# A two-layer hybrid trunk on one core: queries turned one place later, one weighing ahead of the next unit's sums, a head's norm behind the low part of the head ahead, and the FFN's norm rows a triple later

## The chip, the core and the metric

The kernel runs on one core of a Trainium2 chip. Five engines work side by side, each through its own list of instructions, in order: TensorE (PE, matrix products and transposes), VectorE (DVE), ScalarE (ACT), GpSimd (POOL) and SyncE (SP, which starts the weight transfers). They wait for each other through semaphores. The metric is the device time of one execution in microseconds (us); the lower, the better.

## The reference

The input is x, 512 tokens by 1024 features in float32. Two layers are applied. Layer 0 is a Mamba-2 mixer and a ConvFFN; then one shared K/V projection is made; layer 1 is differential attention over it and a second ConvFFN. The parts that the change touches:

```python
def conv_ffn(x, ln_g, up_w, conv_w, conv_b, down_w):
    u = causal_dwconv(rms_norm(x, ln_g) @ up_w, conv_w, conv_b)
    gate, up = u[..., :FFN_DIM], u[..., FFN_DIM:]
    return (jax.nn.silu(gate) * up) @ down_w
...
    q = (rms_norm(x, ln_g) @ q_w).reshape(b, s, ATT_HEADS, 2, ATT_HEAD_DIM)
    q = rms_norm(q, q_norm_g)
    lam = jnp.exp(jnp.sum(lv[0] * lv[1])) - jnp.exp(jnp.sum(lv[2] * lv[3])) + lam_init
...
        logits = jnp.einsum('bqhcd,bkhcd->bhcqk', qblk, k).astype(jnp.float32) * scale
        logits = logits + bias[None, :, None]
        logits = jnp.where(dist >= 0, logits, -jnp.inf)
        p = jax.nn.softmax(logits, axis=-1)
        attn = p[:, :, 0] - lam * p[:, :, 1]
        return jnp.einsum('bhqk,bkhd->bqhd', attn.astype(v.dtype), v)
...
    o = rms_norm(o, subln_g) * (1.0 - lam_init)
    return o.reshape(b, s, V_TOTAL) @ out_w
```

There are 8 attention heads, each with two softmax maps of width 64 and a value width of 128; the FFN is 2816 wide. Before the mixers and FFNs stands an RMS norm whose factor per token is taken out of the product: the product is made with the raw stream, and its result is multiplied by the factor.

## The kernel before

**Products.** Every float32 operand is split in a high and a low part, and each product is three matmuls, high by high, high by low and low by high (`mm3`, L196 to L198; with the tokens on the output's partitions in `proj`, L997 to L999). Such a group is called a triple here. Features lie on the 128 partitions in 8 blocks, the 512 tokens along the free axis. Weights come in chunks by SP's queue into `wr_...`; ACT makes the high part `wh_...` (L147, L165), DVE the low part `wl_...` (L151, L166), two chunks ahead of their use.

**PSUM.** Eight banks: four called "mm" for the long products, four called "aux" for everything short (transposes, logits, values). Each kind is handed out in a ring, so a new use of a bank waits until the engine that reads its last use is done.

**The FFN.** It goes through 22 pairs of blocks, gate `g` and up `u`. A block is 8 triples into an mm bank (`ps_g...`, `ps_u...`), then DVE multiplies by the norm row (`uu`/L874), and three taps of a convolution follow. The norm row is made inside the first pair: `tr_nf` (sum of squares, transposed, then the inverse root on DVE, L428) is turned by four transposes into `al_nf` (L455) and copied by ACT into `nr_f` (L503). On PE the four transposes of `al_nf` stand within the first u block.

**Attention.** k, q and v are projected in two halves of four heads (k0, q0, v0, k1, q1, v1). A finished q projection is squared and summed, gets its norm (L1019 to L1028, tile `knq`), and is transposed in four banks `ktq` (L1035), each evacuated by ACT into `qT` (L1036). When this happens is said by a pair of places, such as `((0, 3), (2, 1))`: the first two banks behind block (k0 = 0, bank 3) of the projection that follows, the next two behind (2, 1). One bank of a step of two features' blocks is six matmuls.

A head is three units, `PARTS = ((0, 1), (2,), (3,))`, of the token blocks given; unit 6_1 is head 6, part 1. A unit runs through: logits (PE L1079 into two aux banks; DVE's maxima L1085, negated at L1088; ACT's exponentials L1093, which also sum), weighing (`weigh`: DVE's reciprocal `rc` L1100, `sm` L1102, and the difference of the two maps `lg` L1106), turning (PE's transposes `at` L1114, copied by ACT L1115) and values (PE `po` L1125, ACT `ot` L1128). After its last unit a head gets its norm (`normed_out`: squares `osq` by ACT at L1135, DVE's sum `so` L1136, the inverse root L434 to L439 with two small ACT instructions at L435 and L436, and the scaling `ot` L1138) and later its transposition (`turned_out`: PE `oT` L1144, ACT's high part `oh` L1147, DVE's low part `ol` L1148), then the output projection, whose results DVE adds to the stream (`xT`, L510).

**What sets the order.** In the attention stage PE's order is written out by hand: between the steps of the units a generator `fill` puts pieces of the projections. The other engines' order comes from a scheduler at build time, which goes by its own estimates of when inputs are ready; `tc.issue_after(x)` puts what stands under it behind x in that order. Each engine then follows its list strictly.

Of the kernel before, what the change touches and what calls it, by code (L numbers as in the profile page):

```python
# [39 lines left out]
def trunk_kernel(ctx: ExitStack, tc, x, ssm_ln_g, ssm_in_w, ssm_conv_w, ssm_conv_b, ssm_dt_bias,  # L40
# [443 lines left out]
    class Norm:  # L484
# [15 lines left out]
        def row(self):  # L500
            ps = along_tokens(self.col(), "n" + self.name)
            r = self.pl.tile([P, T], F32, tag="nr", name="nr_" + self.name)
            act.activation(r, ps, AF.Copy)  # L503
            return r
# [351 lines left out]
    def ffn(l, norm, bp, gnext, nnext):  # L856
        with tc.tile_pool(name="ffn_h%d" % l, bufs=1) as hp, tc.tile_pool(name="ffn%d" % l, bufs=1) as fp:
            rr = []

            def u_block(j, p):  # L860
                key = "%s%d_%d" % ("gu"[j], l, p)
                wh, wl = chunk(key)
                ps = mm_bank("ps_" + key)
                for k in range(KB):
                    mm3(ps, wh[:, k, :], wl[:, k, :], xgh[k], xgl[k], k == 0, k == KB - 1)
                if not rr:
                    rr.append(norm.row())
                r = rr[0]
                col = lambda t: cf[l][:, 88 * j + 22 * t + p:88 * j + 22 * t + p + 1]
                u = fp.tile([P, T], F32, tag="u", name="u" + key, bufs=3)  # L870
                v = fp.tile([P, T], F32, tag="v%d" % j, name="v" + key, bufs=3)
                if nnext is None and key in ("g1_1", "u1_1"):
                    residual(j)
                dve.tensor_tensor(out=u, in0=ps, in1=r, op=ALU.mult)  # L874
                act.activation(v, u, AF.Identity, bias=col(3), scale=col(2))
                for s in range(1, 3):
                    dve.scalar_tensor_tensor(out=v[:, s:], in0=u[:, :T - s], scalar=col(2 - s),
                                             in1=v[:, s:], op0=ALU.mult, op1=ALU.add)
                return v
# [50 lines left out]
            for p0, p1 in ((0, HALF), (HALF, NPAIR)):  # L930
                last = p1 == NPAIR
                hh, hl = [], []
                for p in range(p0, p1):
                    ga = u_block(0, p)
                    act.activation(ga, ga, AF.Silu)
                    up = u_block(1, p)
# [28 lines left out]
    with tc.tile_pool(name="att_o", bufs=1) as op_, tc.tile_pool(name="att", bufs=1) as ap:  # L965
# [23 lines left out]
        def proj(key, evac):  # L989
            pss = [mm_bank("ps_%s_%d" % (key, b)) for b in range(NT)]  # L990
            for k0 in range(0, KB, 2):
                wh, wl = chunk("%s_%d" % (key, k0))
                for b in range(NT):
                    ts = slice(b * P, (b + 1) * P)
                    for k in range(k0, k0 + 2):
# [3 lines left out]
                        pe.matmul(pss[b], xgl[k][:, ts], wh[:, k - k0, :], start=False, stop=sp_)  # L999
                    if b % 2:  # L1000
                        if late and late[0][0] == (k0, b):
                            late.pop(0)[1]()
# [47 lines left out]
        class Unit:  # L1050
# [45 lines left out]
            def weigh(self):  # L1096
# [7 lines left out]
                for j, i in enumerate(self.ii):  # L1104
                    c = slice(self.off[j], self.off[j] + (i + 1) * P)
                    dve.scalar_tensor_tensor(out=p[0][:, c], in0=p[1][:, c], scalar=sm[:, j, 1:2],  # L1106
                                             in1=p[0][:, c], op0=ALU.mult, op1=ALU.add)
# [32 lines left out]
        def turned_out(h, st):  # L1140
            ot = st["ot"]
            ps = aux_bank("oT%d" % h)
            for i in range(NT):
# [4 lines left out]
            dve.scalar_tensor_tensor(out=ol_, in0=ps, scalar=c2[:, 50:51], in1=oh_.bitcast(F32),  # L1148
                                     op0=ALU.mult, op1=ALU.subtract)
# [48 lines left out]
        with tc.manual_schedule(engines={mybir.EngineType.PE}):  # L1198
            run(qk("k0", kT[0], 48, ((2, 1), (2, 3))))
            run(qk("q0", qT[0], 49, ((0, 3), (2, 1))))  # L1200
            fill = chain(vproj("v0", 0), qk("k1", kT[1], 48, ((0, 3), (2, 3))), qk("q1", qT[1], 49, ((0, 3), (2, 1))), vproj("v1", 1),
# [7 lines left out]
            ots = []  # L1209
# [3 lines left out]
            def values(t):  # L1213
                u = us[t]
                u.values()
                if u.part == len(PARTS) - 1:
                    normed_out(u.h, u.st)
                    ots.append([t + 4 + u.h // 4, u])
# [26 lines left out]
            for places in [(2, 2), (2, 2), (2, 2), 2, 2, (2, 2), 2, 2, 2, 1, 1, 1, 2, 1, 2, 1, 2, 1, 2, 2, 1, 1, 1]:  # L1245
                if isinstance(places, tuple):
                    weigh_to(t)
                    turn_to(t - 1)
                    values_to(t - 2)
                    turn_to(t)  # L1250
                    next(fill)
                    out_of(t + 1)
                    values_to(t)
                    next(fill)
# [9 lines left out]
                if t < n:  # L1264
                    us[t].logits()
                weigh_to(t)
                values_to(t - 2)
                for i in range(places):
                    next(fill)
                    if i == 0 and (places > 1 or t > n):  # L1270
                        out_of(t)
                t += 1
# [40 lines left out]
```

## Time and profile before

| what | value |
|---|---|
| time, median of 3 runs | 1351.42 us (1350.94 to 1352.56) |
| profiled execution | 1352.13 us, its span 1350.4 us |
| PE busy | 1342.4 us, 99% of the span |
| DVE, ACT, POOL busy | 68%, 48%, 8% |
| last chain: PE, DVE, ACT | 93%, 3%, 2% |

A row of the timeline reads: start in us, length in us, engine, line, operation, output<-inputs, shapes, count; in brackets how long the engine idled before it, and whose instruction ended that. Lengths of matmuls are modelled and overlap the next one's start, so distances are taken from start to start. Line numbers are those of the kernel before; in the changed one the same instructions of the attention stand some ten lines further on.

### The profile page before, as it was taken

The page shows a single profiled execution, that of the slowest core. Times are in us where ns is not written, and L with a number is a line of the kernel's source. Part 1 is how long each engine was busy: PE and PEld are TensorE (multiplying, and loading weights), DVE is VectorE, ACT ScalarE, POOL GpSimd, SP SyncE. Part 2 cuts the span into 40 slices and gives each one's busy share as a digit, 9 for nine tenths or more (in the row PEclk, how much of TensorE's full clock was granted, in tenths as well). Part 3 has the DMA queues.
Part 4 walks back from the last instruction along what each step waited for, and adds up shares of the span by engine and source line. Part 5 has one row for each costly group of instructions (what it writes and reads, how often), then busy time and mean ns, then how long its engine had stood idle before and what let it go on. Part 6 is the DMA issues. An engine that isn't in the chain of part 4 may idle for free.

```text
span 1350.4 us, 16886 instructions
## 1 busy us (share of the span) xinstructions
PE 1342.4 (99%) x6423; PEld 1097.3 (81%) x6423; DVE 915.0 (68%) x1525; ACT 646.2 (48%) x1060; POOL 106.3 (8%) x142
## 2 busy tenths in 40 slices
PE   9999999999999999999999999999999999999998
PEld 7878788888888888888888887777888888888887
DVE  4989888788877774267754556778777773367743
ACT  5696553742444442234433556777654442134430
POOL 6230400200110000000001200000110000000000
PEclk9999999999999999999999999999999999999999
DMA  7453433432333333333323422221232332333322
GB/s 204 143 166 90 138 109 110 133 94 71 94 94 94 94 98 105 94 94 94 100 80 102 133 78 89 69 86 36 76 92 87 103 94 94 94 104 99 94 94 78
DMA packets 179825, 134.98 MB, mean 100 GB/s; under 512 B 6492, under 2 KB 163552, under 8 KB 179744
## 3 DMA queue, kind: packets, MB, share of 16 engines
q1 hardware_dynamic: 173872, 120.73, 29.7%
q0 software_dynamic: 4592, 12.08, 2.8%
q10 hardware_dynamic: 1280, 1.10, 0.2%
q8 instruction: 50, 0.82, 0.2%
q14 instruction: 31, 0.25, 0.1%
HBM read 131.64 MB, written 2.25 MB: 99 GB/s over the span
## 4 chain that ended last, share of the span: by engine, by line
PE 93%; DVE 3%; ACT 2%; issue 1%; DMA 0%; POOL 0%; SPq 0%; ACTq 0%; DVEq 0%
PE ps_g L197 6%; PE ps_g L198 6%; PE ps_g L196 6%; PE ps_u L198 6%; PE ps_u L196 6%; PE ps_u L197 6%; PE ps_in L196 4%; PE ps_in L197 4%; PE ps_in L198 4%; PE ps_d L198 3%; PE ps_d L196 3%; PE ps_d L197 3%; PE ps_d L915 3%; PE ps_d L914 3%; PE ps_d L913 3%; PE ps_o L197 2%
## 5 line engine op out<-in xcount | busy, mean ns | idle before, releaser
L196 PE MATMUL ps_u<-xgh,wh_u 128*128 128x512 f32 x352 | 137.6, 391 | 0.0
L197 PE MATMUL ps_g<-xgl,wh_g 128*128 128x512 f32 x352 | 137.2, 390 | 0.0
L196 PE MATMUL ps_g<-xgh,wh_g 128*128 128x512 f32 x352 | 137.2, 390 | 0.0
L198 PE MATMUL ps_u<-xgh,wl_u 128*128 128x512 f32 x352 | 137.2, 390 | 0.0
L198 PE MATMUL ps_g<-xgh,wl_g 128*128 128x512 f32 x352 | 137.2, 390 | 0.0
L197 PE MATMUL ps_u<-xgl,wh_u 128*128 128x512 f32 x352 | 137.1, 390 | 0.0
L196 PE MATMUL ps_in<-xgh,wh_in 128*128 128x512 f32 x304 | 126.4, 416 | 0.0
L151 DVE TENSOR_TENSOR wl_d<-wr_d,wh_d 128x1024 fp32r<-128x1024 f32 (+1 forms) x46 | 54.2, 1179 | 96.9 <-ACT wh_d L147 96.7
L197 PE MATMUL ps_in<-xgl,wh_in 128*128 128x512 f32 x304 | 119.5, 393 | 0.0
L198 PE MATMUL ps_in<-xgh,wl_in 128*128 128x512 f32 x304 | 119.4, 393 | 0.0
L147 ACT ACTIVATE wh_d<-wr_d 128x1024 fp32r<-128x1024 f32 (+1 forms) x46 | 47.1, 1024 | 130.6 <-PE ps_d L915 62.4
L874 DVE TENSOR_TENSOR uu<-ps_u,nr_f 128x512 f32<-128x512 f32 x44 | 30.4, 692 | 78.0 <-PE ps_u L198 77.9
L940 ACT ACTIVATE hh<-vg 128x512 fp32r<-128x512 f32 x44 | 27.8, 632 | 114.9 <-DVE vg L939 114.9
L197 PEld LDWEIGHTS ps_g<-xgl,wh_g 128*128 128x128 f32 x352 | 66.1, 188 | 13.9 <-DVE xgl L413 0.3
L198 PEld LDWEIGHTS ps_g<-xgh,wl_g 128*128 128x128 f32 x352 | 66.1, 188 | 13.7
L198 PEld LDWEIGHTS ps_u<-xgh,wl_u 128*128 128x128 f32 x352 | 66.1, 188 | 13.7
L197 PEld LDWEIGHTS ps_u<-xgl,wh_u 128*128 128x128 f32 x352 | 66.2, 188 | 13.6
L196 PEld LDWEIGHTS ps_g<-xgh,wh_g 128*128 128x128 f32 x352 | 66.1, 188 | 13.6
L196 PEld LDWEIGHTS ps_u<-xgh,wh_u 128*128 128x128 f32 x352 | 66.1, 188 | 13.5
L147 ACT ACTIVATE wh_g<-wr_g 128x1024 fp32r<-128x1024 f32 x44 | 46.7, 1062 | 51.6 <-PE ps_u L197 32.3
L198 PE MATMUL ps_d<-hh,wl_d 128*128 128x512 f32 x176 | 68.6, 390 | 0.0
L196 PE MATMUL ps_d<-hh,wh_d 128*128 128x512 f32 x176 | 68.6, 390 | 0.0
(359 smaller groups left out, 3180.5 us busy)
## 6 DMA issues: line engine op xcount, KB each, us to landing
wr_g<-in_ffn_up_w_dram SPq DMA_DIRECT2D x44, 512.0 KB, 3.7
wr_u<-in_ffn_up_w_dram SPq DMA_DIRECT2D x44, 512.0 KB, 3.7
wr_d<-in_ffn_down_w_dram SPq DMA_DIRECT2D x42, 512.0 KB, 3.6
wr_in<-in_ssm_in_w_dram SPq DMA_DIRECT2D x40, 512.0 KB, 3.8
m<-cumd POOLq DMA_DIRECT2D x16, 512.0 KB, 5.0
wr_out<-in_ssm_out_w_dram SPq DMA_DIRECT2D x16, 512.0 KB, 3.3
wr_k<-in_kv_w_dram SPq DMA_DIRECT2D x8, 512.0 KB, 3.7
wr_q<-in_q_w_dram SPq DMA_DIRECT2D x8, 512.0 KB, 3.6
```

The source lines that it names most:

```text
L147: return act.activation(self.wh[:, :self.n], self.raw[:, :self.n], AF.Copy)
L151: return eng.tensor_tensor(out=self.wl[:, :self.n], in0=self.raw[:, :self.n], in1=self.wh[:, :self.n].bitcast(F32), op=ALU.subtract)
L196: pe.matmul(ps, wh, xh, start=start, stop=False)
L197: pe.matmul(ps, wh, xl, start=False, stop=False)
L198: return pe.matmul(ps, wl, xh, start=False, stop=stop).ins
L874: dve.tensor_tensor(out=u, in0=ps, in1=r, op=ALU.mult)
L913: pe.matmul(pss[b], hh[k][:, ts], wh[:, k - k0, :], start=k == 0, stop=False)
L914: pe.matmul(pss[b], hh[k][:, ts], wl[:, k - k0, :], start=False, stop=False)
L915: pe.matmul(pss[b], hl[k][:, ts], wh[:, k - k0, :], start=False, stop=k == stop)
L940: act.activation(h, ga, AF.Copy)
```

## The change

It makes five edits, none of which adds or removes an instruction of an engine:

1. The norm row of both FFNs: the four transposes `al_nf` stand behind the seventh triple of the first u block instead of the sixth. For this, `u_block` is split into `products` and `taps`.
2. The transposes of q0 move from the places `((0, 3), (2, 1))` to `((2, 0), (2, 2))` of v0's projection, those of q1 to `((2, 0), (2, 1))` of v1's; the place is looked up behind each bank instead of behind every second.
3. Unit 6_0 (number 18 of 24) is weighed ahead of the logits of unit 6_1, whose maxima are put behind the last instruction of that weighing.
4. `normed_out` comes after the next piece of the fill instead of directly behind the values, and, in the later heads, behind the low part `ol` of the head that was turned last.
5. As a result of these, the scheduler's order of DVE and ACT changes in a few more places. The orders of POOL and SP stay as they are.

On PE in layer 0's FFN, within the first u block (`ps_u0_0`), before:

```order
L196 MATMUL ps_u0_0_3645<-xgh5_91,wh_u0_0_3522 128x512
L197 MATMUL ps_u0_0_3645<-xgl5_99,wh_u0_0_3522 128x512
L198 MATMUL ps_u0_0_3645<-xgh5_91,wl_u0_0_3523 128x512
L455 MATMUL al_nf0_3625<-ident_77,tr_nf0_3609 128x128 x4
L196 MATMUL ps_u0_0_3645<-xgh6_92,wh_u0_0_3522 128x512
L197 MATMUL ps_u0_0_3645<-xgl6_100,wh_u0_0_3522 128x512
L198 MATMUL ps_u0_0_3645<-xgh6_92,wl_u0_0_3523 128x512
```

and in the changed kernel:

```order
L196 MATMUL ps_u0_0_3631<-xgh5_91,wh_u0_0_3522 128x512
L197 MATMUL ps_u0_0_3631<-xgl5_99,wh_u0_0_3522 128x512
L198 MATMUL ps_u0_0_3631<-xgh5_91,wl_u0_0_3523 128x512
L196 MATMUL ps_u0_0_3631<-xgh6_92,wh_u0_0_3522 128x512
L197 MATMUL ps_u0_0_3631<-xgl6_100,wh_u0_0_3522 128x512
L198 MATMUL ps_u0_0_3631<-xgh6_92,wl_u0_0_3523 128x512
L455 MATMUL al_nf0_3653<-ident_77,tr_nf0_3609 128x128 x4
```

The four transposes have passed one triple, that of feature block 6. Layer 1 shows the same.

On ACT, where q1's four banks `ktq1` are evacuated, beside head 2's norm (`osq2`, `so2`) and a weight chunk of v1, before:

```order
L1135 ACTIVATE osq2_7471<-ot2_7245 128x512
L165 ACTIVATE wh_v1_6_7510<-wr_v1_6_7508,c2_103 128x512
L1036 ACTIVATE qT1_6145<-ktq1_0_7496,c2_103 128x4x128
L1036 ACTIVATE qT1_6145<-ktq1_1_7502,c2_103 128x4x128
L435 ACTIVATE so2_7472<-rsm_o2_7475 128x4
L165 ACTIVATE wh_v1_6_7510<-wr_v1_6_7508,c2_103 128x512
L436 ACTIVATE so2_7472<-so2_7472 128x4
L1036 ACTIVATE qT1_6145<-ktq1_2_7528,c2_103 128x4x128
L1036 ACTIVATE qT1_6145<-ktq1_3_7534,c2_103 128x4x128
L1115 ACTIVATE at3_1_7540<-at3_1_7541 128x384
```

and in the changed kernel:

```order
L1146 ACTIVATE osq2_7483<-ot2_7245 128x512
L165 ACTIVATE wh_v1_6_7498<-wr_v1_6_7496,c2_103 128x512 x2
L435 ACTIVATE so2_7484<-rsm_o2_7487 128x4
L1046 ACTIVATE qT1_6145<-ktq1_0_7510,c2_103 128x4x128
L436 ACTIVATE so2_7484<-so2_7484 128x4
L1046 ACTIVATE qT1_6145<-ktq1_1_7516,c2_103 128x4x128
L1046 ACTIVATE qT1_6145<-ktq1_2_7528,c2_103 128x4x128
L1046 ACTIVATE qT1_6145<-ktq1_3_7534,c2_103 128x4x128
L1126 ACTIVATE at3_1_7540<-at3_1_7541 128x384
```

The first small activation of head 2's norm stood behind the first two evacuations and now stands ahead of all four; both halves of the weight are ahead of it, and the second small activation stands between the first two evacuations.

On DVE, from the scaling of head 4's output on, at the beginning of head 6, before:

```order
L1138 TENSOR_TENSOR ot4_7756<-ot4_7756,so4_7866 128x512
L1085 ISA lg6_1_0_7954,mx6_1_7952<-lg6_1_0_7956,tb6_7890 128x384
L1085 ISA mx6_1_7952 128x1
L1085 ISA lg6_1_1_7955,mx6_1_7952<-lg6_1_1_7957,tb6_7890 128x384
L1085 ISA mx6_1_7952 128x1
L1100 RECIPROCAL rc6_0_7965<-sm6_0_7895 128x4
L1088 TENSOR_SCALAR mx6_1_7952<-mx6_1_7952 128x2
L1102 SCALAR_TENSOR_TENSOR sm6_0_7895<-sm6_0_7895,nlam_108,rc6_0_7965 128x2
L1106 SCALAR_TENSOR_TENSOR lg6_0_0_7896<-lg6_0_1_7897,sm6_0_7895,lg6_0_0_7896 128x128
L1106 SCALAR_TENSOR_TENSOR lg6_0_0_7896<-lg6_0_1_7897,sm6_0_7895,lg6_0_0_7896 128x256
L510 TENSOR_TENSOR xT_85<-ps_ao0_2_7938,xT_85 128x512
```

and in the changed kernel:

```order
L1149 TENSOR_TENSOR ot4_7756<-ot4_7756,so4_7872 128x512
L1110 RECIPROCAL rc6_0_7952<-sm6_0_7895 128x4
L1112 SCALAR_TENSOR_TENSOR sm6_0_7895<-sm6_0_7895,nlam_108,rc6_0_7952 128x2
L1116 SCALAR_TENSOR_TENSOR lg6_0_0_7896<-lg6_0_1_7897,sm6_0_7895,lg6_0_0_7896 128x128
L1116 SCALAR_TENSOR_TENSOR lg6_0_0_7896<-lg6_0_1_7897,sm6_0_7895,lg6_0_0_7896 128x256
L1095 ISA lg6_1_0_7959,mx6_1_7957<-lg6_1_0_7961,tb6_7890 128x384
L1095 ISA mx6_1_7957 128x1
L1095 ISA lg6_1_1_7960,mx6_1_7957<-lg6_1_1_7962,tb6_7890 128x384
L1095 ISA mx6_1_7957 128x1
L510 TENSOR_TENSOR xT_85<-ps_ao0_2_7938,xT_85 128x512
L1098 TENSOR_SCALAR mx6_1_7957<-mx6_1_7957 128x2
```

The weighing of unit 6_0 (its four instructions on `rc6_0`, `sm6_0` and `lg6_0`) has passed the maxima of unit 6_1, and the addition of `ps_ao0_2` to the stream stands ahead of their negation.

On DVE, further on in head 6, behind the weighing of unit 6_2 (head 5's norm `so5`, head 4's low part `ol4`), before:

```order
L1106 SCALAR_TENSOR_TENSOR lg6_2_0_7990<-lg6_2_1_7991,sm6_2_7989,lg6_2_0_7990 128x512
L1136 TENSOR_REDUCE so5_8012<-osq5_8011 128x4
L1148 SCALAR_TENSOR_TENSOR ol4_8037<-oT4_8031,c2_103,oh4_8036 128x512
L434 TENSOR_SCALAR rsm_o5_8015<-so5_8012 128x4
L510 TENSOR_TENSOR xT_85<-ps_ao0_3_8024,xT_85 128x512
```

and in the changed kernel:

```order
L1116 SCALAR_TENSOR_TENSOR lg6_2_0_7990<-lg6_2_1_7991,sm6_2_7989,lg6_2_0_7990 128x512
L1159 SCALAR_TENSOR_TENSOR ol4_8024<-oT4_8018,c2_103,oh4_8023 128x512
L1147 TENSOR_REDUCE so5_8028<-osq5_8027 128x4
L510 TENSOR_TENSOR xT_85<-ps_ao0_3_8011,xT_85 128x512
L434 TENSOR_SCALAR rsm_o5_8031<-so5_8028 128x4
```

The low part and the sum of squares have changed places. Of the diff, all is shown:

```diff
--- before.py
+++ after.py
@@ -497,8 +497,8 @@
 
             (dve if k == KB - 1 else pool).tensor_tensor(out=self.acc, in0=self.acc, in1=sq, op=ALU.add)
 
-        def row(self):
-            ps = along_tokens(self.col(), "n" + self.name)
+        def row(self, col):
+            ps = along_tokens(col, "n" + self.name)
             r = self.pl.tile([P, T], F32, tag="nr", name="nr_" + self.name)
             act.activation(r, ps, AF.Copy)
             return r
@@ -857,14 +857,19 @@
         with tc.tile_pool(name="ffn_h%d" % l, bufs=1) as hp, tc.tile_pool(name="ffn%d" % l, bufs=1) as fp:
             rr = []
 
-            def u_block(j, p):
+            def products(j, p, c=None):
                 key = "%s%d_%d" % ("gu"[j], l, p)
                 wh, wl = chunk(key)
                 ps = mm_bank("ps_" + key)
                 for k in range(KB):
-                    mm3(ps, wh[:, k, :], wl[:, k, :], xgh[k], xgl[k], k == 0, k == KB - 1)
-                if not rr:
-                    rr.append(norm.row())
+                    last = mm3(ps, wh[:, k, :], wl[:, k, :], xgh[k], xgl[k], k == 0, k == KB - 1)
+                    if c is not None and k == KB - 2:
+                        with tc.issue_after(last):
+                            rr.append(norm.row(c))
+                return ps
+
+            def taps(j, p, ps):
+                key = "%s%d_%d" % ("gu"[j], l, p)
                 r = rr[0]
                 col = lambda t: cf[l][:, 88 * j + 22 * t + p:88 * j + 22 * t + p + 1]
                 u = fp.tile([P, T], F32, tag="u", name="u" + key, bufs=3)
@@ -931,9 +936,14 @@
                 last = p1 == NPAIR
                 hh, hl = [], []
                 for p in range(p0, p1):
-                    ga = u_block(0, p)
+                    ps = [products(0, p)]
+                    if not rr:
+                        ps.append(products(1, p, norm.col()))
+                    ga = taps(0, p, ps[0])
                     act.activation(ga, ga, AF.Silu)
-                    up = u_block(1, p)
+                    if len(ps) == 1:
+                        ps.append(products(1, p))
+                    up = taps(1, p, ps[1])
                     h = hp.tile([P, T], F32R, tag="hh", name="hh%d_%d" % (l, p), bufs=HALF + 1)
                     w = hp.tile([P, T], F32R, tag="hl", name="hl%d_%d" % (l, p), bufs=HALF + 1)
                     dve.tensor_tensor(out=ga, in0=ga, in1=up, op=ALU.mult)
@@ -997,9 +1007,9 @@
                         pe.matmul(pss[b], xgh[k][:, ts], wh[:, k - k0, :], start=st, stop=False)
                         pe.matmul(pss[b], xgh[k][:, ts], wl[:, k - k0, :], start=False, stop=False)
                         pe.matmul(pss[b], xgl[k][:, ts], wh[:, k - k0, :], start=False, stop=sp_)
+                    if late and late[0][0] == (k0, b):
+                        late.pop(0)[1]()
                     if b % 2:
-                        if late and late[0][0] == (k0, b):
-                            late.pop(0)[1]()
                         if k0 == 0 and b == 3:
                             if not rts:
                                 tc.keep_in_program_order(
@@ -1103,8 +1113,9 @@
                                          in1=rc[:, :, 1:2], op0=ALU.mult, op1=ALU.mult)
                 for j, i in enumerate(self.ii):
                     c = slice(self.off[j], self.off[j] + (i + 1) * P)
-                    dve.scalar_tensor_tensor(out=p[0][:, c], in0=p[1][:, c], scalar=sm[:, j, 1:2],
-                                             in1=p[0][:, c], op0=ALU.mult, op1=ALU.add)
+                    self.weighed = dve.scalar_tensor_tensor(
+                        out=p[0][:, c], in0=p[1][:, c], scalar=sm[:, j, 1:2], in1=p[0][:, c],
+                        op0=ALU.mult, op1=ALU.add).ins
 
             def turn(self):
                 tag = self.tag
@@ -1145,8 +1156,8 @@
             oh_ = op_.tile([P, T], F32R, tag="oh", name="oh%d" % h, bufs=6)
             ol_ = op_.tile([P, T], F32R, tag="ol", name="ol%d" % h, bufs=6)
             act.activation(oh_, ps, AF.Copy, scale=c2[:, 50:51])
-            dve.scalar_tensor_tensor(out=ol_, in0=ps, scalar=c2[:, 50:51], in1=oh_.bitcast(F32),
-                                     op0=ALU.mult, op1=ALU.subtract)
+            state["ol"] = dve.scalar_tensor_tensor(out=ol_, in0=ps, scalar=c2[:, 50:51], in1=oh_.bitcast(F32),
+                                                   op0=ALU.mult, op1=ALU.subtract).ins
             return oh_, ol_
 
         os = []
@@ -1197,8 +1208,8 @@
 
         with tc.manual_schedule(engines={mybir.EngineType.PE}):
             run(qk("k0", kT[0], 48, ((2, 1), (2, 3))))
-            run(qk("q0", qT[0], 49, ((0, 3), (2, 1))))
-            fill = chain(vproj("v0", 0), qk("k1", kT[1], 48, ((0, 3), (2, 3))), qk("q1", qT[1], 49, ((0, 3), (2, 1))), vproj("v1", 1),
+            run(qk("q0", qT[0], 49, ((2, 0), (2, 2))))
+            fill = chain(vproj("v0", 0), qk("k1", kT[1], 48, ((0, 3), (2, 3))), qk("q1", qT[1], 49, ((2, 0), (2, 1))), vproj("v1", 1),
                          attn_out(0, None, range(KB)))
             us = []
             for h in range(AH):
@@ -1206,7 +1217,7 @@
                 us += [Unit(h, part, st) for part in range(len(PARTS))]
             n = len(us)
 
-            ots = []
+            ots, valued_heads = [], []
             for _ in range(3):
                 next(fill)
 
@@ -1214,8 +1225,13 @@
                 u = us[t]
                 u.values()
                 if u.part == len(PARTS) - 1:
+                    valued_heads.append(u)
+                    ots.append([t + 4 + u.h // 4, u])
+
+            def norm_heads():
+                while valued_heads:
+                    u = valued_heads.pop(0)
                     normed_out(u.h, u.st)
-                    ots.append([t + 4 + u.h // 4, u])
 
             def out_of(t):
                 if ots and ots[0][0] <= t:
@@ -1247,10 +1263,12 @@
                     weigh_to(t)
                     turn_to(t - 1)
                     values_to(t - 2)
+                    norm_heads()
                     turn_to(t)
                     next(fill)
                     out_of(t + 1)
                     values_to(t)
+                    norm_heads()
                     next(fill)
                     us[t].logits()
                     us[t + 1].logits()
@@ -1261,7 +1279,11 @@
                     t += 2
                     continue
                 turn_to(t - 1)
-                if t < n:
+                if t == n - 5:
+                    weigh_to(t)
+                    with tc.issue_after(us[t - 1].weighed):
+                        us[t].logits()
+                elif t < n:
                     us[t].logits()
                 weigh_to(t)
                 values_to(t - 2)
@@ -1269,6 +1291,10 @@
                     next(fill)
                     if i == 0 and (places > 1 or t > n):
                         out_of(t)
+                    if valued_heads and os:
+                        with tc.issue_after(state["ol"]):
+                            norm_heads()
+                    norm_heads()
                 t += 1
             assert next(fill, None) is None
             last_out(norm1)
```

## The prediction, made before the changed kernel was run

> **What bounds the kernel now.** I read the busy table first, then the shares of the chain that ended last, then the cores, and from there the timeline around every place that the change touches.
>
> ```profile
> PE 1342.4 (99%) x6423; PEld 1097.3 (81%) x6423; DVE 915.0 (68%) x1525; ACT 646.2 (48%) x1060; POOL 106.3 (8%) x142
> ...
> PE 93%; DVE 3%; ACT 2%; issue 1%; DMA 0%; POOL 0%; SPq 0%; ACTq 0%; DVEq 0%
> ...
> core 0: 1350.4 us, clock 1.000
> ```
>
> TensorE (PE) is busy 99% of the span, 93% of the last chain is its own work, and its clock is never throttled. No instruction of PE is removed or added, so the change can only close gaps in which PE waits for DVE or ACT, and those hold 5% of the chain. What a gap is worth I take from the distance between two PE starts, because a PE row's length overlaps its successor: in the next fence the transposes at 386.90 start 0.23 us behind the product at 386.67, though that row says 0.39. Each moved place is compared with the same sequence of instructions somewhere else where nothing is waited for.
>
> **Edit 1, the FFN's norm row, one triple later (twice).**
>
> ```profile
> 386.67 0.39 PE L198 MATMUL ps_g<-xgh,wl_g 128*128 128x512 f32 x1
> 386.90 0.60 PE L445 MATMUL tr_nf<-ident,nacc_f 128*128 128x128 f32 x4
> 387.25 0.47 PE L196 MATMUL ps_u<-xgh,wh_u 128*128 128x512 f32 x1
> ...
> 391.22 0.39 PE L198 MATMUL ps_u<-xgh,wl_u 128*128 128x512 f32 x1
> ...
> 391.76 0.62 PE L455 MATMUL al_nf<-ident,tr_nf 128*128 128x128 f32 x4 [0.16 <-DVE tr_nf L428]
> 392.14 0.47 PE L196 MATMUL ps_u<-xgh,wh_u 128*128 128x512 f32 x1
> ...
> 992.75 0.39 PE L198 MATMUL ps_u<-xgh,wl_u 128*128 128x512 f32 x1
> ...
> 993.59 0.48 PE L196 MATMUL ps_u<-xgh,wh_u 128*128 128x512 f32 x1
> ```
>
> In layer 0 the four transposes stretch the product-to-product distance to 392.14 − 391.22 = 0.92. Four transposes that wait for nothing (the tr_nf row) make it 0.58. Gap: 0.34. In layer 1 it is 0.84 − 0.58 = 0.26. One triple is 3 × 0.23 = 0.69, and the row al_nf was released some 0.3 us after the point at which PE asked for it, so it is ready when the triple is over: I take the whole, 0.34 + 0.26 = 0.60. The ends are 0 (the wait comes back) and 0.60. What is late next: the copy of the row and the first tap of the first two blocks, by 0.69 − 0.34 = 0.35; their PSUM banks come round again only two blocks of 24 products (2 × 5.5 us) later, which covers it. The transposes are counted in both places, no DMA moves, and SP and POOL keep their orders.
>
> **Edit 2, the queries' transposes.** For q0:
>
> ```profile
> 792.52 2.50 DVE L1028 TENSOR_TENSOR knq<-knq,ssq 128x512 f32<-128x512 f32 x4
> 792.82 0.39 PE L999 MATMUL ps_v<-wh_v,xgl 128*128 128x512 f32 x1
> ...
> 794.34 0.48 PE L997 MATMUL ps_v<-wh_v,xgh 128*128 128x512 f32 x1
> ...
> 796.95 0.39 PE L999 MATMUL ps_v<-wh_v,xgl 128*128 128x512 f32 x1
> ...
> 797.97 0.48 PE L997 MATMUL ps_v<-wh_v,xgh 128*128 128x512 f32 x1
> ```
>
> The first pair is met while DVE still scales the rows (0.6 us each from 792.52); it takes 1.52, the second pair 1.02. Gap: 0.50. Both first rows are scaled by 793.8, and PE, six products (1.4 us) later than its present 793.05, asks at 794.4. I take all of it; ends 0 and 0.50. The first logits that read them stand behind 18 more products (4.1 us), which covers the later evacuations. For q1:
>
> ```profile
> 886.00 0.39 PE L999 MATMUL ps_v<-wh_v,xgl 128*128 128x512 f32 x1
> ...
> 887.55 0.48 PE L997 MATMUL ps_v<-wh_v,xgh 128*128 128x512 f32 x1
> ...
> 889.66 0.20 ACT L435 ACTIVATE so<-rsm_o 128x4 f32<-128x4 f32 x1 [0.72 <-DVE rsm_o L434]
> 889.77 0.71 ACT L165 ACTIVATE wh_v<-wr_v,c 128x512 fp32r<-128x512 f32 x1
> ...
> 891.03 1.26 ACT L1036 ACTIVATE qT<-ktq,c 128x512 f32<-128x512 f32 x2 [0.45 <-PE ktq L1035]
> ...
> 891.68 1.00 PE L1079 MATMUL lg<-kT,qT 64*128 64x128 f32 x8
> ...
> 892.62 0.94 PE L1125 MATMUL po<-vt,at 128*128 128x128 f32 x6
> ```
>
> The same gap, 887.55 − 886.00 − 1.02 = 0.53, closes. But ACT's order now has the first activation of head 2's norm ahead of all four evacuations, and that one cannot start before 889.66, since DVE delivers its input just then, and by the order no earlier in the changed kernel. The four evacuations (0.62 each, two for 1.26) and the second small activation (about 0.1 of start distance, 889.77 against 889.66) then run from 889.8 to 892.4. The transposes use PSUM banks in a ring of four, so at3_1, the two banks of the logits and po3_0 need the evacuations one after the other: the last frees po3_0 at 892.4 + 0.1 = 892.5, against 892.62 now. I take 0.10; ends 0 and 0.53.
>
> ACT's strict order is what decides this, and the trace shows it: the weight half at 889.77 had its input and an idle engine, and stood 0.72 us behind the small activation. The Trainium skill, page "Perfetto Trace Analysis", section "Tensor Engine Instruction (MATMUL, LD_WEIGHTS)", says that ACT and DVE are strict FIFO; the trace agrees at this row (0.72 us). Were evacuations able to pass, this term would be 0.53 and the sum of all 2.5. The same section says that a matmul's profiled end is estimated, not observed; going by the bracketed waits alone the recoverable time here would be 0.16 at 391.76 and 0.33 at 932.47 (edit 3), about half of the 0.34 and 0.73 that the starts give there.
>
> **Edit 3, head 6's first weighing ahead of the next maxima.**
>
> ```profile
> 929.95 0.69 DVE L1138 TENSOR_TENSOR ot<-ot,so 128x512 f32<-128x512 f32 x1
> ...
> 931.50 0.17 DVE L1100 RECIPROCAL rc<-sm 128x4 f32<-128x4 f32 x1
> 931.74 0.40 PE L198 MATMUL ps_ao<-oh,wl_ao 128*128 128x512 f32 x1
> 931.97 0.75 DVE L1106 SCALAR_TENSOR_TENSOR lg<-lg,sm,lg 128x128 f32<-128x128 f32 x2
> 932.47 0.74 PE L1114 MATMUL at<-ident,lg 128*128 128x128 f32 x3 [0.33 <-DVE lg L1106]
> 933.14 1.13 PE L1079 MATMUL lg<-kT,qT 64*128 64x512 f32 x4
> ...
> 938.18 0.40 PE L198 MATMUL ps_ao<-oh,wl_ao 128*128 128x512 f32 x1
> ...
> 938.85 0.93 PE L1079 MATMUL lg<-kT,qT 64*128 64x128 f32 x8
> ```
>
> Three transposes and the switch take 933.14 − 931.74 = 1.40 where the weighed logits are late, and 938.85 − 938.18 = 0.67 where they are not. Gap: 0.73. Now the reciprocal follows the head's output at 930.6, 0.9 us earlier, so the weighing ends near 931.8 instead of 932.7, and PE asks at 932.0. I take 0.73; ends 0 and 0.73. Late next: the two maxima of unit 6_1, by the three small instructions and the pair (about 1.2 us); they end near 932.7, and the bank that they free is asked for near 932.9, where PE now arrives early. That is narrow, and is part of the loss below.
>
> **Edit 4, norm behind the head ahead's low part.**
>
> ```profile
> 909.96 0.93 PE L1079 MATMUL lg<-kT,qT 64*128 64x128 f32 x8
> 910.82 0.94 PE L1125 MATMUL po<-vt,at 128*128 128x128 f32 x6
> ...
> 911.52 0.69 DVE L1138 TENSOR_TENSOR ot<-ot,so 128x512 f32<-128x512 f32 x1
> ...
> 917.92 0.60 PE L1144 MATMUL oT<-ident,ot 128*128 128x128 f32 x4
> ...
> 939.12 0.74 DVE L1148 SCALAR_TENSOR_TENSOR ol<-oT,c,oh 128x512 fp32r<-128x512 f32 x1
> 939.92 0.94 PE L1125 MATMUL po<-vt,at 128*128 128x128 f32 x6
> ```
>
> po6_0 needs the bank that the low part of head 4 reads last: 939.92 − 938.85 = 1.07 behind the logits, against 910.82 − 909.96 = 0.86. Gap: 0.21; the low part now comes 0.6 us earlier, ahead of the sum of squares, so I take all. Head 3's norm ends later (after up to two us of maxima); its output at 912.2 is read at 917.92, which covers it, so 0.
>
> **The loss.** Behind head 6 PE is then 0.73 + 0.21 = 0.94 ahead, and DVE must follow:
>
> ```profile
> 943.52 0.17 DVE L1088 TENSOR_SCALAR mx<-mx 128x4 f32<-128x4 f32 x1
> ...
> 946.09 0.75 DVE L1106 SCALAR_TENSOR_TENSOR lg<-lg,sm,lg 128x128 f32<-128x128 f32 x2
> ...
> 947.46 0.49 PE L1114 MATMUL at<-ident,lg 128*128 128x128 f32 x3
> ```
>
> The weighing of head 7 ends at 946.84 and is asked for at 947.46. PE will ask at 946.5. By the order the negation at 943.52 comes about 0.46 earlier (one output norm left the stretch ahead of it, a weight's low part moved in), so the weighing ends at 946.4: slack 0.1. I take a loss of 0.1 here; ends 0 and 0.94 (the whole gain given back).
>
> **Sum.** 0.60 + 0.50 + 0.10 + 0.73 + 0.21 − 0.10 = 2.0. Against the profiled execution's own 1352.1 (span 1350.4 and 1.7 around it) that is 1350.1. That execution lies 0.7 above the median of the runs shown, 1351.42, so the forecast for the median is 1349.4. All gaps closed with no loss: 0.60 + 0.50 + 0.53 + 0.73 + 0.21 = 2.6.
>
> **Rivals.** *Everything comes, and a little more.* The 0.67 that I took as undisturbed for three transposes still holds 0.44 beside the product; at edit 1's unwaited rate (0.35 for four) it would be 0.26, so up to 0.2 more lies in at6_0, and about as much in edit 2's 1.02 (eight transposes, 0.79 beside the product against 0.70). Sum 2.6 to 3.0, with 2.9 the time is 1348.5. For: the DVE chain gets shorter there too. Against: q1's replay.
>
> *DVE becomes the limit from head 6 on.* Slack 0.1 becomes a wait, and the 0.94 is given back at head 7. Left are 0.60 + 0.50 + 0.10 = 1.2, thus 1350.2. For: the narrow slacks above, and 5% of the chain already lies on DVE and ACT. Against: DVE is busy only 68%.
>
> *ACT holds q1, and the kernel is slower.* The four evacuations now hang on the input of head 2's norm. Each us by which DVE delivers that one later than 889.66 stalls PE's logits by one us. It outweighs the other 1.9 from 2.0 us on; with 5 us late the time is 1354.4. For: the rows above show ACT waiting there already. Against: no DVE instruction is put ahead of it in the order, and nothing else in the change delays it.
>
> *The gaps are not waits but the price of a switch between shapes*, and return wherever the transposes stand. Then the time is 1351.4. Against: the same switches without a wait take 0.58, 1.02 and 0.67.
>
> **How the numbers follow.** Forecast 44%, with its own range 1348.6 to 1350.3 (q1's 0.4 more, or the 0.94 mostly returned). Everything and more: 32%. DVE as limit: 12%. ACT holds q1: 6%. No waits: 6%. About 0.2% (2.7 us) is what a measurement of this kernel can tell from no change, so faster means below 1348.7: two thirds of the second case and a tenth of the first, 0.26. Slower is the fourth case alone, 0.06. The rest, 0.68, lies within. The range goes from 1347.9 (all, the little more, and the runs' own scatter of half a us) to 1351.3, which leaves out the slower case and half of the last.
>
> **What would show it.** In the changed kernel: al_nf without a wait in both layers; first pairs of q0 and q1 at 1.02 between products; the small activation ahead of four evacuations, and po3_0 near 892 when shifted by the earlier gains; at6_0 at 0.67; po6_0 at 0.86 behind the logits; at7_0 with at most 0.1 of wait. I am wrong if new waits stand at lg4_0, lg6_2 or at7_0 that together exceed 0.6, or if the span moves by more than 3 us, which no gap that I found can pay.

## The result, and the profile after

The changed kernel takes 1349.18 us (median of 20 runs, 1348.26 to 1350.41) against 1351.36 us (20 runs, 1350.48 to 1352.56) of the kernel before: 2.2 us less, a ratio of 0.9984 with a 95% interval of 0.9978 to 0.9990. The forecast was 1349.4. The changed kernel's page, by busy time, last chain and core:

```profile
PE 1341.6 (100%) x6423; PEld 1097.6 (81%) x6423; DVE 914.1 (68%) x1525; ACT 646.0 (48%) x1060; POOL 105.8 (8%) x142
...
PE 94%; DVE 2%; ACT 2%; DMA 0%; issue 0%; POOL 0%; SPq 0%; ACTq 0%; DVEq 0%
...
core 0: 1347.7 us, clock 1.000
```

The work is the same, the chain lost a point of DVE, and the span is 2.7 us shorter. To see where, I subtract the start of each PE instruction in the profile of before from the start of the same instruction in the profile after. That offset is flat over long stretches (within 0.02 us over the 300 us of the last FFN) and steps only at a few places, which make up the ledger below:

| place | forecast | step, changed kernel | step with that edit alone |
|---|---|---|---|
| mixer, first 330 us | 0 | -0.73 | (see the last section) |
| edit 1, FFN 0's norm row | -0.34 | -0.37 | -0.37 |
| edit 2, q0 | -0.50 | -0.51 | -0.50 |
| k1's first transposes | not foreseen | +0.19 | +0.13 with edit 4, -0.01 with edit 2 |
| edit 2, q1 | -0.10 | -0.03 | -0.04 |
| edit 3, at6_0 | -0.73 | -0.75 | -0.75 |
| edit 4, po6_0 | -0.21 | -0.23 | -0.23 |
| head 7 | +0.10 | -0.01 | +0.01 with edit 3 |
| edit 1, FFN 1's norm row | -0.26 | -0.28 | -0.27 |
| sum without the mixer | -2.04 | -1.99 | |

Five places close as foreseen: both norm rows, q0, at6_0 and po6_0. PE around both norm rows and around q0's first pair, in the changed kernel:

```profile
391.17 0.39 PE L198 MATMUL ps_u<-xgh,wl_u 128*128 128x512 f32 x1
391.39 0.60 PE L455 MATMUL al_nf<-ident,tr_nf 128*128 128x128 f32 x4
391.75 0.48 PE L196 MATMUL ps_u<-xgh,wh_u 128*128 128x512 f32 x1
...
793.08 0.39 PE L1009 MATMUL ps_v<-wh_v,xgl 128*128 128x512 f32 x1
793.31 1.03 PE L1045 MATMUL ktq<-ident,knq 128*128 128x128 f32 x8
794.10 0.48 PE L1007 MATMUL ps_v<-wh_v,xgh 128*128 128x512 f32 x1
...
990.99 0.39 PE L198 MATMUL ps_u<-xgh,wl_u 128*128 128x512 f32 x1
...
991.57 0.48 PE L196 MATMUL ps_u<-xgh,wh_u 128*128 128x512 f32 x1
```

From the product ahead of the transposes to the one behind them it is 0.58 at the norm row in both layers (0.92 and 0.84 before), and the transposes' row shows no wait; across q0's pair it is 1.02 (1.52 before). At head 6 and head 7, DVE and PE:

```profile
929.09 0.18 DVE L1110 RECIPROCAL rc<-sm 128x4 f32<-128x4 f32 x1
...
930.29 0.39 PE L198 MATMUL ps_ao<-oh,wl_ao 128*128 128x512 f32 x1
930.52 0.49 PE L1125 MATMUL at<-ident,lg 128*128 128x128 f32 x3
...
936.63 0.93 PE L1089 MATMUL lg<-kT,qT 64*128 64x128 f32 x8
937.49 0.94 PE L1136 MATMUL po<-vt,at 128*128 128x128 f32 x6
...
944.06 0.75 DVE L1116 SCALAR_TENSOR_TENSOR lg<-lg,sm,lg 128x128 f32<-128x128 f32 x2
...
945.02 0.49 PE L1125 MATMUL at<-ident,lg 128*128 128x128 f32 x3
```

The weighing of 6_0 starts 1.2 us ahead of PE's last product; at6_0 follows that product after 0.23, and po6_0 stands 0.86 behind the logits. At head 7 the weighing ends at 944.81 and is asked for at 945.02. The slack is 0.2, where 0.1 was forecast, and nothing is lost.

At q1 the first pair closes and the time comes back behind the second, as replayed; the row before the last is PE's weight load for po3_0:

```profile
885.94 0.39 PE L1009 MATMUL ps_v<-wh_v,xgl 128*128 128x512 f32 x1
...
886.96 0.48 PE L1007 MATMUL ps_v<-wh_v,xgh 128*128 128x512 f32 x1
...
888.19 0.39 PE L1009 MATMUL ps_v<-wh_v,xgl 128*128 128x512 f32 x1
...
888.25 0.20 ACT L435 ACTIVATE so<-rsm_o 128x4 f32<-128x4 f32 x1 [1.25 <-DVE rsm_o L434]
888.36 0.67 ACT L1046 ACTIVATE qT<-ktq,c 128x512 f32<-128x512 f32 x1
...
889.03 1.83 ACT L1046 ACTIVATE qT<-ktq,c 128x512 f32<-128x512 f32 x3
...
889.76 1.50 PE L1089 MATMUL lg<-kT,qT 64*128 64x128 f32 x8
...
891.18 0.74 PEld L1136 LDWEIGHTS po<-vt,at 128*128 128x128 f32 x6 [0.33 <-ACT qT L1046]
891.18 0.94 PE L1136 MATMUL po<-vt,at 128*128 128x128 f32 x6
```

The first pair takes 1.02 (1.55 before). But ACT idles 1.25 us for head 2's norm with the evacuations queued behind it, the logits stretch to 1.50 from 1.00, and po3_0 waits for the last evacuation.

### The profile page after: what moved, and what is told of

The parts are those of the page before. It is cut to its first block, busy times and chain, and to the rows that moved or that the text cites. A ratio compares the mean times of both kernels' runs of the same rounds, so it can differ in the third digit from the quotient of the medians.

```text
span 1347.7 us, 16888 instructions
## 1 busy us (share of the span) xinstructions
PE 1341.6 (100%) x6423; PEld 1097.6 (81%) x6423; DVE 914.1 (68%) x1525; ACT 646.0 (48%) x1060; POOL 105.8 (8%) x142
## 4 chain that ended last, share of the span: by engine, by line
PE 94%; DVE 2%; ACT 2%; DMA 0%; issue 0%; POOL 0%; SPq 0%; ACTq 0%; DVEq 0%
PE ps_u L196 6%; PE ps_g L197 6%; PE ps_g L196 6%; PE ps_u L198 6%; PE ps_g L198 6%; PE ps_u L197 6%; PE ps_in L196 4%; PE ps_in L197 4%; PE ps_in L198 4%; PE ps_d L196 3%; PE ps_d L197 3%; PE ps_d L198 3%; PE ps_d L920 3%; PE ps_d L918 3%; PE ps_d L919 3%; PE ps_o L197 2%
## 5 line engine op out<-in xcount | busy, mean ns | idle before, releaser
L197 PE MATMUL ps_d<-hl,wh_d 128*128 128x512 f32 x176 | 68.5, 389 | 0.0
```

The costliest lines, as they stand in the source:

```text
L197: pe.matmul(ps, wh, xl, start=False, stop=False)
```

## The experiments

Times alone cannot tell these edits apart: the runs of one kernel lie 1 to 3 us apart, and the intervals of a ratio are about 0.09% (1.2 us) to either side. The verdicts below rest on the steps of the offsets.

**Each edit alone, on the kernel before.** First the norm rows:

```diff
-                if not rr:
-                    rr.append(norm.row())
+                    if c is not None and k == KB - 2:
+                        with tc.issue_after(last):
+                            rr.append(norm.row(c))
```

> The kernel before with edit 1 alone (both FFN norm rows one triple later). My theory, that the two places held waits of PE for DVE: the two gaps close, 0.37 and 0.28 us in the trace, about 0.65 together, time 1350.7; the transposes show no wait, and nothing else moves by more than 0.1. Rival, that the distance is the price of switching between shapes: the same distance appears one triple later, time 1351.4.

Measured: 1350.89 against 1351.88 in the same session (0.9993, 0.9983 to 1.0002). The steps are -0.37 and -0.27, everything between them flat within 0.05. The gaps were waits; they did not travel with the instructions.

```diff
-            run(qk("q0", qT[0], 49, ((0, 3), (2, 1))))
+            run(qk("q0", qT[0], 49, ((2, 0), (2, 2))))
-            ... qk("q1", qT[1], 49, ((0, 3), (2, 1))) ...
+            ... qk("q1", qT[1], 49, ((2, 0), (2, 1))) ...
```

> The kernel before with edit 2 alone (q0 and q1). My theory: q0's place gains 0.50 in the trace; q1's first pair gains 0.5 and loses it again before po3_0, because ACT has head 2's norm ahead of the evacuations, net 0.0 to 0.1. In the trace of the full change k1's transposes give back about 0.15 to 0.19 of what q0 gained, which I had not foreseen; if that is caused by PE coming there 0.5 earlier, it shows here too, so 0.3 to 0.4 in all, time 1351.0. Rival, that the loss at k1 comes from another edit or from the scatter of one execution: 0.5 to 0.6 in all.

Measured: 1350.90 against 1351.88 (0.9995, 0.9985 to 1.0004). Steps: q0 -0.50, k1 -0.01, q1 -0.04. So my first reading of the loss at k1, that q0's gain turned into a wait there, fell: PE came to k1 0.5 us earlier and lost nothing.

```diff
-                if t < n:
+                if t == n - 5:
+                    weigh_to(t)
+                    with tc.issue_after(us[t - 1].weighed):
+                        us[t].logits()
+                elif t < n:
                     us[t].logits()
```

> The kernel before with edit 3 alone (unit 6_0 weighed ahead of the maxima of 6_1). My theory: at6_0 gains 0.73 to 0.75 in the trace and nothing of it is lost at heads 6 and 7, time 1350.7. Rival, DVE as the limit from head 6 on: half or more of it comes back as a wait at po6_0 or at head 7; at po6_0 this could show here more than in the full change, since head 4's low part still stands behind the sum of squares, and then 0.3 to 0.5 remains.

Measured: 1351.05 against 1351.88 (0.9994, 0.9985 to 1.0003). Step at at6_0: -0.75; after that the offset stays within 0.03 to the end. With this edit alone, DVE is not the limit behind head 6. Without edit 4, PE's row at po6_0 names what it still waits for there, the low part of head 4:

```profile
938.71 0.94 PE L1126 MATMUL po<-vt,at 128*128 128x128 f32 x6 [0.16 <-DVE ol L1149]
```

```diff
-                    normed_out(u.h, u.st)
+                    valued_heads.append(u)
...
+                    if valued_heads and os:
+                        with tc.issue_after(state["ol"]):
+                            norm_heads()
+                    norm_heads()
```

> The kernel before with edit 4 alone (a head's norm behind the fill and behind the low part of the head ahead). My theory: the distance from the logits to po6_0 goes from 1.07 to 0.86, a gain of 0.2, time 1351.2, not to be told from the kernel before by its time. Rival: the norms that now come later hold PE up at a head's transposition, a loss of up to 0.5.

Measured: 1351.45 against 1351.88 (0.9996, 0.9987 to 1.0006). po6_0 gains 0.23 as expected. And k1's transposes lose 0.13 although no transposes of q or k were moved: the loss belongs to this edit, at a head that I had not looked at. This profile also loses 0.40 in FFN 0, which edit 4 does not touch (last section).

Added up, the steps of the four edits alone give -2.03 and those of the changed kernel -1.99, so the edits hardly affect one another. The four differences of the times would add up to 3.2 us, which the width of their intervals allows.

**The changed kernel again, and the norm rows asked for earlier.**

The first is the changed kernel without any edit.

> The changed kernel once more, as the measure for the three beside it. About 1349.2, and by the ledger of places 2.0 below the kernel before; the 0.7 that the profile of the changed kernel showed in the mixer, whose instructions are the same, should be different here if it is scatter of one execution, and the same if the change caused it.

Measured: 1349.41 against 1351.51 (0.9987, 0.9979 to 0.9996), the steps behind the mixer again -2.02 in all (-0.70 to -2.72), with +0.15 at k1. In the mixer it is again -0.70, which by what I had written would speak for the change as its cause. But the four kernels with one edit each, three of which touch nothing but the attention, show -0.15 to -0.63 there; it is the profile of the kernel before that lies high (last section).

The second, an edit of the changed kernel:

```diff
-                    if c is not None and k == KB - 2:
+                    if c is not None and k == KB - 4:
```

> The changed kernel with both FFN norm rows behind the fifth triple of the u block in place of the seventh (the kernel before has them behind the sixth). If PE waits there for DVE's tr_nf, whose time is fixed, each place loses what the seventh gained and one triple more: 0.37 + 0.69 and 0.28 + 0.69, together 2.0 above the changed kernel, and the rows of the transposes show the wait. If the distance is the price of a switch between shapes, the place makes no difference: 0.0.

Measured: 1350.35 against 1351.51, and 1349.41 for the changed kernel beside it. Neither 2.0 nor 0.0: the steps at the two norm rows are -0.01 and +0.03, so 0.67 is lost against the changed kernel. The test did not do what I wanted. In the FFN PE's order is the scheduler's, and the edit only sets an earliest place; it put the rows behind the sixth triple, where they stood before. Thus it is an undoing of edit 1 inside the changed kernel, and shows that the edit is worth the same there as alone (0.64 to 0.67). A place still earlier was not tried.

**Why q1's move is worth nothing.** Its undoing, and its repair:

```diff
-            ... qk("q1", qT[1], 49, ((2, 0), (2, 1))) ...
+            ... qk("q1", qT[1], 49, ((0, 3), (2, 1))) ...
```

> The changed kernel with q1's transposes back at ((0, 3), (2, 1)), q0's left where the change put them. If q1's move is worth nothing because of ACT's order, the offsets behind po3_0 are those of the changed kernel within 0.1, though the first pair waits 0.5 again. If q1's move is what carries the gain, it is 0.5 slower from there on.

Measured: 1349.16, one run. The step over q1's place is +0.02, where the changed kernel has -0.03: the move is worth 0.05.

```diff
+            def rest():
                 rsqrt_act(so, ap, "o%d" % h, [P, NT], P)
                 dve.tensor_tensor(out=ot, in0=ot, in1=so.unsqueeze(2).to_broadcast([P, NT, P]), op=ALU.mult)
+            if h == 2:
+                state["rest"] = rest
+            else:
+                rest()
...
+            def norm_rest():
+                if "q1" in state and "rest" in state:
+                    with tc.issue_after(state.pop("q1")):
+                        state.pop("rest")()
```

Here `state["q1"]` is q1's last evacuation.

> The changed kernel with the later part of head 2's norm (from the inverse root on) behind q1's four evacuations on ACT. My theory, that ACT's order makes q1's move worth nothing: the evacuations follow the transposes at once, po3_0 starts 0.4 to 0.6 earlier relative to the same products, and the time falls by as much, to about 1348.7. Rival, that the logits there are bound by the evacuations' own length or by at3_1: 0.0 to 0.1. A third way: head 2's output is normalized about a us later and its transposes wait, which would take the gain back there.

Measured: 1349.08 against 1351.51 (0.9982, 0.9973 to 0.9991). ACT and PE at q1:

```profile
887.12 1.25 ACT L1046 ACTIVATE qT<-ktq,c 128x512 f32<-128x512 f32 x2
...
888.41 0.39 PE L1009 MATMUL ps_v<-wh_v,xgl 128*128 128x512 f32 x1
...
889.27 1.27 ACT L1046 ACTIVATE qT<-ktq,c 128x512 f32<-128x512 f32 x2 [0.91 <-PE ktq L1045]
890.43 0.20 ACT L435 ACTIVATE so<-rsm_o 128x4 f32<-128x4 f32 x1
...
890.86 0.94 PE L1138 MATMUL po<-vt,at 128*128 128x128 f32 x6
```

The evacuations run as soon as their transposes are there, and po3_0 starts 2.45 behind the product at 888.41 instead of 2.99 behind the one at 888.19 in the changed kernel. The step over the place is -0.55, and the offset is flat behind it: head 2's later output costs nothing. The order of ACT was the cause. Whether freeing ACT would gain as much with q1's transposes in their old place was not run, so the 0.5 is shown for the two together.

**What k1 loses.** ACT at head 0's norm and PE at k1's first pair, in the kernel before:

```profile
830.59 0.69 ACT L1128 ACTIVATE ot<-po,rc 128x128 f32<-128x128 f32 x2
831.18 0.62 ACT L1135 ACTIVATE osq<-ot 128x512 f32<-128x512 f32 x1
...
852.85 0.39 PE L999 MATMUL ps_q<-wh_q,xgl 128*128 128x512 f32 x1
853.08 1.06 PE L1035 MATMUL ktk<-ident,knk 128*128 128x128 f32 x8
853.89 0.48 PE L997 MATMUL ps_q<-wh_q,xgh 128*128 128x512 f32 x1
```

and in the changed kernel:

```profile
828.99 0.95 ACT L1139 ACTIVATE ot<-po,rc 128x128 f32<-128x128 f32 x3
829.82 0.63 ACT L1146 ACTIVATE osq<-ot 128x512 f32<-128x512 f32 x1
...
851.24 0.39 PE L1009 MATMUL ps_q<-wh_q,xgl 128*128 128x512 f32 x1
851.47 1.20 PE L1045 MATMUL ktk<-ident,knk 128*128 128x128 f32 x8
852.42 0.47 PE L1007 MATMUL ps_q<-wh_q,xgh 128*128 128x512 f32 x1
```

By edit 4 one more evacuation (the second of unit 1_0) runs ahead of head 0's squares: they start 0.83 behind the first evacuation instead of 0.59. The pair at k1, 20 us later, takes 1.18 instead of 1.04. Is that one instruction the cause? Head 0's norm alone is put back:

```diff
-                    valued_heads.append(u)
+                    if u.h:
+                        valued_heads.append(u)
+                    else:
+                        normed_out(u.h, u.st)
```

> The changed kernel with head 0's norm alone put back directly behind its values, so that on ACT its squares stand ahead of the second of unit 1_0's two evacuations again, as before the change. If the 0.15 to 0.19 that k1's transposes lose comes from these squares starting one evacuation (0.26 us) later, at the head of a chain over DVE and ACT without slack, the loss there goes to 0.0 to 0.05, and 0.15 is gained in all. If it comes from q0's earlier arrival or from another head's norm, it stays.

Measured: 1349.36 against 1351.49 (0.9985, 0.9976 to 0.9994). ACT and PE there:

```profile
829.07 0.69 ACT L1139 ACTIVATE ot<-po,rc 128x128 f32<-128x128 f32 x2
829.66 0.62 ACT L1146 ACTIVATE osq<-ot 128x512 f32<-128x512 f32 x1
...
851.33 0.39 PE L1009 MATMUL ps_q<-wh_q,xgl 128*128 128x512 f32 x1
...
852.36 0.48 PE L1007 MATMUL ps_q<-wh_q,xgh 128*128 128x512 f32 x1
```

The pair takes 1.03, the step over k1's place is 0.00 where it was +0.19, and the rest of edit 4 keeps its gain (-0.23 at po6_0). The squares' place it is. The delay can be followed: head 0's sum `so` starts on DVE at 830.49 in the changed kernel and at 830.31 here, k1's scaling `knk`, which the pair's transposes read, at 850.60 and 850.54, while PE comes to the product ahead of the pair at 851.24 and 851.33. Relative to PE the scaling is 0.15 later in the changed kernel. (In FFN 0 this profile, too, loses 0.41 that no edit explains; the norm row behind that place still takes 0.58. See the last section.)

**Both repairs.** Two ways: k1's pair one place later as well, or head 0's norm put back.

```diff
-            ... qk("k1", kT[1], 48, ((0, 3), (2, 3))) ...
+            ... qk("k1", kT[1], 48, ((2, 0), (2, 3))) ...
```

> The same as the run with q1's evacuations freed, and with k1's first transposes at the place (2, 0) in place of (0, 3) too. If the wait at k1's transposes is what q0's gain turned into, this closes it (0.15 to 0.19 and whatever wait stood there already), so 0.6 to 0.8 below the changed kernel, about 1348.5. Rival: k1's wait moves on to its evacuations and the next unit's logits, as with q1; then no more than the run before.

Measured: 1349.01 against 1351.51 (0.9981, 0.9973 to 0.9990); steps behind the mixer -2.71 in all, k1's -0.02 and q1's -0.55.

The other kernel joins the two edits already shown, the freed evacuations and head 0's norm put back:

> The run with q1's evacuations freed, and head 0's norm put back as in the run beside it. If both causes are as told, the two gains add up: 0.55 at q1's place and 0.15 at k1's, 0.7 below the changed kernel in the trace, about 1348.6. If k1's loss returns at q1's place (the chain of DVE and ACT being late in any case), 0.5 to 0.6.

Measured: 1348.81 against 1351.49 (0.9980, 0.9971 to 0.9989); steps behind the mixer -2.62, k1's +0.03 and q1's -0.55. By the ledger these two are 0.6 to 0.7 below the changed kernel (the second 0.6, where 0.7 was expected); by their times 0.4 (against 1349.41 in the same session), or 0.55 (against 1349.36 of the run with head 0 put back), which no interval here separates. They have the lowest medians of all that ran, but 1349.08 with the evacuations alone is not told apart from them by its time.

## Why the prediction was right, and where it was not

**Edit 1** held: both gaps closed, 0.37 and 0.28 for 0.34 and 0.26, and the later taps cost nothing. **q0** held to 0.01.

**q1** held in its mechanism: ACT's strict order gives the first pair's gain back. The size was off: 0.03 rather than 0.10. The four evacuations end at 889.03 + 1.83 = 890.86, 1.43 ahead of the 892.29 (891.03 + 1.26) of the kernel before, and PE stood 1.42 ahead when it came there, so nothing is left. What I mis-sized is the step from the last evacuation's end to po3_0: the replay allowed 0.1, and it is 0.32 to 0.33 in the kernel before, in the changed one and in the repaired one (890.54 to 890.86). The forecast's own rows for the kernel before already showed the 0.33. The evacuations ended 0.1 sooner than the replay had them (892.28 in its time, against 892.4), which took back a part of the error. The rival that would have had ACT hold the kernel back on balance did not happen, since head 2's norm input was not late.

**Edit 3** held to 0.02, **edit 4's** gain at po6_0 too.

**Edit 4's cost was put at 0, and that step failed.** I checked head 3, found its output covered for 5 us, and concluded for all heads. Head 0's squares, one ACT instruction of 0.26 us later, lead a chain of ACT and DVE with little slack that ends at k1's transposes 20 us on: +0.13 with the edit alone, +0.19 in the full change (0.14 at the pair itself, 0.05 within the next ten us) and +0.15 in its repeat, 0.00 with head 0 put back.

**The loss at head 7** (0.10) did not come: slack 0.2, no wait. The two errors cancel almost, 0.10 too much and 0.19 too little; that the sum was right to 0.05 is in part luck.

The case in which *everything comes and a little more* was kept away by q1 and k1, 0.5 and 0.2, and its little more hardly came: at6_0 and q0 gained 0.02 and 0.01 beyond their gaps. *DVE as the limit* is excluded by the slack of 0.2 at head 7 in the changed kernel and by the flat offset behind edit 3 alone, and *the price of a switch* by the norm rows alone.

## What to carry to other kernels

When one engine is nearly always busy, compare the distance between two of its starts around a suspected wait with the same sequence elsewhere: the difference was the gain to within 0.03 us at five places of six (both norm rows, q0, at6_0, po6_0). At the sixth, q1, the gap of 0.53 closed too, but the time came back a few us later, so the engine that reads the result has to be followed as well. An edit that moves a step "to later" must be followed for every instance that it moves, in the order of each engine, since one short instruction put ahead of the head of a tight chain shows as a wait 20 us later. Where a moved transpose gains on TensorE, look at what stands ahead of its evacuation on the in-order engine behind it; moving that aside was worth ten times the move itself.

## What the runs showed of the hardware

The -0.73 of the mixer is a sum of steps at instructions that the change does not touch: -0.50 up to 146 us, in several pieces that were not followed further, -0.79 at the place below, and +0.56 at 236 us. DVE, GpSimd (POOL) and PE at the middle one, in the kernel before and then in the changed one:

```profile
149.00 1.68 DVE L657 TENSOR_TENSOR xe<-xd,dec 128x512 f32<-128x512 f32 x1
149.02 1.10 POOL L632 TENSOR_SCALAR_AFFINE_SELECT m<-m 128x1024 f32<-128x1024 f32 x1
...
149.86 0.40 PE L196 MATMUL ps_o<-yh,wh_out 128*128 128x512 f32 x1
150.82 1.10 PE L682 MATMUL st<-xe,bt 128*128 128x512 f32 x2 [0.56 <-DVE xe L657]
```

```profile
148.50 0.68 DVE L657 TENSOR_TENSOR xe<-xd,dec 128x512 f32<-128x512 f32 x1
148.59 1.54 POOL L632 TENSOR_SCALAR_AFFINE_SELECT m<-m 128x1024 f32<-128x1024 f32 x1
...
149.36 0.40 PE L196 MATMUL ps_o<-yh,wh_out 128*128 128x512 f32 x1
149.60 1.02 PE L682 MATMUL st<-xe,bt 128*128 128x512 f32 x2
```

The same multiplication took 1.68 us in the one execution and 0.68 in the other, and PE waited 0.7 us for it. In the 13 profiles of this study PE waits at this place in 4 (0.24 to 0.66 by the bracket), among them kernels with and without the change, so it is scatter of an execution.

POOL's rows show what the multiplication meets. Where it takes 1.68, the select of POOL beside it takes 1.10; where it takes 0.68 or 0.69 (the other 9 profiles), the select takes 1.23 to 1.68. At 236 us the same two instructions meet again: in the changed kernel the multiplication takes 1.51 and the select 1.09, in the kernel before 0.69 and 1.56. At both places, in all 13 profiles, exactly one of the two is long, so they do not run side by side there; which one has to wait differs from execution to execution. The 0.40 and 0.41 in FFN 0, with edit 4 alone and with head 0 put back, come with the same picture: three of DVE's low parts `xgl` (L413) take 1.77 to 1.87 beside POOL's sums (L498) of 1.28 to 1.39 in these two profiles, 0.75 beside 1.79 to 1.87 in the others, and PE waits for the last `xgl`. What the two engines contend for is not shown by these runs.

Such scatter means that a difference of two profiled spans (2.7 us here) is not the change's (2.0); the step of the offset, place by place, is.
